# Weight sums of late mixed squares made early by GpSimd, and an eighth mixed square in six groups

## The chip, the cores and the metric

The kernel runs on one core of a Trainium2 chip. The metric is the device time of one execution in microseconds (us), and lower is better. A time stated here without a word beside it is the median of several executions. Times with a place in them ("at 982.89") are counted from the first instruction of one profiled execution.

The engines are named as the profile names them: PE is TensorE (matmuls; PEld its weight loads), DVE is VectorE, ACT is ScalarE, POOL is GpSimd, and SP is SyncE, which here only issues DMAs.

## The reference

One transformer block over 256 tokens of width 4096, in float32:

```python
h = _rmsnorm(x, norm_w)
u = h @ w_in                       # 4096 x 15,440: q, k, v, gates of two mixers
y_ml = rms(mlstm(...)) * sigmoid(ml_o) * silu(ml_z)
y_ns = nsa(...) * silu(ns_z)       # compressed, selected and window attention
x = x + concat([y_ml, y_ns]) @ w_out           # 4096 x 4096
x = x + sigmoid(x @ ple_gate) * (p @ ple_proj)  # 4096 x 4096
```

Nearly all of the arithmetic is in three large products with 256 rows of activations. Everything below is about those.

## The kernel before, in words

**Splits.** Each float32 operand is split into a high part that the fast matmul takes exactly, and a low part, the rest. A product is then three matmuls: high by high, low by high, high by low. The activations ("stationary", tiles `ss0` to `ss7`, `sh` and `sl`) are split once per stage. Each weight tile is loaded by SP into a buffer `raw` (six of them, 128 x 1024 numbers, 512 KB), ACT copies it to `whi` (line 1546, or 1556 for half a tile), and DVE subtracts to get `wlo` (line 1549, or 1559).

**Units.** The whole program is a list of 982 units, one weight tile each, and one loop (from line 1619 on) runs over it. While TensorE is given the matmuls of unit n, the low part of unit n + 3 and the high part of unit n + 4 are made; there are four `whi` and four `wlo`. Loads are issued as raw buffers come free (`load_some`, counted by `held_raw`). Between units, `step` takes one step each of three queues of generators (`urgent`, `fifo`, `third`), in which the attention, the recurrence, the evacuation of results and the preparation of the next activations are written out. All engines run their instructions in this order; only waits on data order them against each other.

**Pair groups and squares.** The weight columns are taken 1024 at a time in "pair groups" (`pair_group`): -9, -8, -7, -10 (early columns of w_in), -6 to -1 (its gate columns), 0 to 3 (w_out), 4 to 7 (ple_gate). The other columns of w_in are "wide groups" (`wide_group`, names such as nq2, 16 units of 12 matmuls each). A pair group has 16 squares kp = 0 to 15, each with 2 x 2 blocks of weights and 2 x 2 blocks of activations. A plain square ("C" in the plan) has two units of 12 matmuls: eight block products of three. A mixed square ("a" and, later, "c") uses seven products in place of eight, in the manner of Strassen and Winograd: units of 3, 6, 6 and 6 matmuls, 21 in all. It needs sums of the activation blocks (`cb`, made by `t_mix` or by `t_stat`) and sums of the weight blocks. Those are made in place, in the two raw buffers that the "a" units loaded, by `sums` (lines 1330, 1332, 1333 and 1335: four DVE additions of 128 x 512). The "c" units then split these sums, and until then the two raw buffers are held. "a" units split half a tile and then a whole one, "c" units two whole ones.

**Plans.** A plan lists the squares of a group. `FULL`, used by groups -5, -4, -3, -2, 1 and 2, has seven mixed squares, and in it 9 and 11 are open at once:

```python
FULL = _plan((0,), (3, 5, 7, (9, 11), 13, 1), (2, 4, 6, 8, 10, 12), (14, 15))
```

That is C0, a3 C2 c3, a5 C4 c5, a7 C6 c7, a9 a11 C8 c9 c11, a13 C10 c13, a1 C12 c1, C14, C15. `SIX` has six mixed squares (groups -9 and -7), and others have fewer.

**Buffers and queues that matter here.** `nat0` to `nat3` (128 x 2 x 1024) hold in turn the input for the norm, the shifted inputs of the compression, keys, mixed activations and the mixers' outputs y, and stand empty in between. `tb` (four small tiles) holds rows of the bias table, loaded on GpSimd's queue (line 520). GpSimd's queue also stores the result (line 1186). All weights go through SP's queue (line 1530), in order.

Of the kernel before, what the change touches and what calls it, by code (L numbers as in the profile page):

```python
# [55 lines left out]
MORE = 1  # L56
# [12 lines left out]
SIX = _plan((0, 1), MIXED, (2, 4, 6, 8, 10, 12), (14, 15))  # L69
TWICE = (3, (5, 7), 9, 11, (13, 1))  # L70
SHIFT = _plan((0,), TWICE, (2, 4, 6, 8, 10), (12, 14, 15))
PLANS = {g: FULL for g in (-5, -4, -3, -2, 1, 2)}
PLANS[-9] = PLANS[-7] = SIX
PLANS[-8] = _plan((0, 1, 2, 3), (5, 7, 9, 11, 13), (4, 6, 8, 10, 12), (14, 15))
CMP_AT = ((-8, 1), (-8, 3), (-8, 5), (-7, 1))
# [17 lines left out]
def hymba_block(ctx: ExitStack, tc: tile.TileContext, a, out: bass.AP):  # L93
# [713 lines left out]
    def mixed_tiles(kp, tag="b"):  # L807
        if tag == "e":
            if kp in (3, 7, 11):
                held["cb"] = wk.tile([128, 2, 2, 4, 128], F32R, tag={3: "a", 7: "nat2", 11: "nat3"}[kp], name="cb")  # L810
            t = held["cb"][:, int(kp in (5, 9, 13))]
            return t[:, 0], t[:, 1]
        if tag == "t":
            return [[wk.tile([128, 2, 128], F32R, tag="tb", name="cb", bufs=4) for _ in range(2)] for _ in range(2)]
        if kp == MORE:
            t = wk.tile([128, 2, 4, 128], F32R, tag="a" if tag == "b" else "b", name="cb")
        elif kp in (3, 5):
            t = wk.tile([128, 2, 4, 128], F32R, tag="qt", name="cb", bufs=2)
        elif kp == 7:
            t = wk.tile([128, 2, 4, 128], F32R, tag="sq", name="cb")  # L820
        elif kp == 13:
            return [wk.tile([128, 4, 128], F32R, tag="pt", name="cb", bufs=2) for _ in range(2)]
        else:
            if kp == 9:
                held["cb"] = wk.tile([128, 2, 2, 4, 128], F32R, tag=tag, name="cb")
            t = held["cb"][:, int(kp == 11)]
        return t[:, 0], t[:, 1]
# [4 lines left out]
    def t_mix(kps, flag, tag="b", gap=0):  # L832

        f = {}
        for i in range(len(kps) + 1):
            if i:
                nc.vector.tensor_sub(cb[kps[i - 1]][1], f[i - 1], cb[kps[i - 1]][0])
                done.add(f"{flag}{kps[i - 1] // 2}m")
            if i == len(kps):
                return  # L840
            c, b = kps[i] // 2, 2 * (kps[i] % 2)
            v = f[i] = stile([128, 4, 128])
            nc.vector.tensor_add(v.rearrange("p a t -> p (a t)"), sh[c][:, b:b + 2].rearrange("p k t -> p (k t)"),
                                 sl[c][:, b:b + 2].rearrange("p k t -> p (k t)"))
            nc.vector.tensor_sub(v[:, 3:0:-2], v[:, 1::-1], v[:, 3:0:-2])
            nc.vector.tensor_sub(v[:, 0], v[:, 0], v[:, 3])
            nc.vector.tensor_sub(v[:, 2], v[:, 2], v[:, 0])
            for _ in range(1 + gap):
                yield
            cb[kps[i]] = mixed_tiles(kps[i], tag)  # L850
            nc.scalar.activation(cb[kps[i]][0], v, AF.Copy)
            for _ in range(1 + gap):
                yield

# [5 lines left out]
    def t_stat(chunks, weighted, bset=1, pace=2, pause=0):  # L860


        def chunk(c, col0, gate, flag):
# [10 lines left out]
            for half in range(2):  # L874
                p, hs = pp[half], slice(2 * half, 2 * half + 2)
                w = [hnw[:, col0 // 128 + 2 * half + i:col0 // 128 + 2 * half + i + 1] for i in range(2)] if scales else None
                if 2 * c + half in MIXED or flag in (f"y{MORE // 2}", f"r{MORE // 2}") and half == MORE % 2:
                    f[half] = stile([128, 4, 128])
                    if scales:
                        for i in range(2):  # L880
                            nc.scalar.activation(f[half][:, 2 * i:2 * i + 2].rearrange("p a t -> p (a t)"), p[:, i],
                                                 AF.Copy, scale=w[i])
                        nc.scalar.activation(sh[c][:, hs].rearrange("p k t -> p (k t)"),
                                             f[half].rearrange("p a t -> p (a t)"), AF.Copy)
                        continue
                    nc.scalar.activation(f[half].rearrange("p a t -> p (a t)"), p.rearrange("p a t -> p (a t)"), AF.Copy)
                if scales:
                    for i in range(2):
                        nc.scalar.activation(sh[c][:, 2 * half + i], p[:, i], AF.Copy, scale=w[i])
                else:  # L890
                    nc.scalar.activation(sh[c][:, hs], p, AF.Copy)
# [360 lines left out]
    def pair_group(g, w, stat):  # L1252
# [125 lines left out]
            unit(w[kp, k], split, mm, kp, post=post)  # L1378

        def a_units(kp):  # L1380
            def split1(r):
                raw[kp] = [r]
                return split_one(r)

            def split2(r):
                raw[kp].append(r)
                low = split_all(r, keep=True)

                def rest():
                    hl = low()  # L1390
                    sums(kp, 0)
                    opened.extend(((kp, 1), (kp, 2)))
                    return hl
                return rest

            def mm1(hi, lo):
                emit(product(oth[0], blocks(kp)(0, 0), stream(hi, 0), stream(lo, 0)))

            def mm2(hi, lo):
                both(product(own[0][0], mixed(kp, 2), stream(hi, 0), stream(lo, 0)),  # L1400
                     product(own[0][1], blocks(kp)(1, 0), stream(hi, 1), stream(lo, 1)))
            unit(w[kp, 0], split1, mm1, kp, True)
            unit(w[kp, 1], split2, mm2, kp, True)

        def c_units(kp, last):
            def mm1(hi, lo):
                both(product(oth[3], mixed(kp, 1), stream(hi, 0), stream(lo, 0)),
                     product(oth[1], mixed(kp, 3), stream(hi, 1), stream(lo, 1)))

            def mm2(hi, lo):  # L1410
                both(product(oth[2], mixed(kp, 0), stream(hi, 0), stream(lo, 0)),
                     product(own[1][1], blocks(kp)(1, 1), stream(hi, 1), stream(lo, 1)))

            def post():
                finish(kp)
                if last:
                    urgent.append(t_x1_oth(g, oth) if 0 <= g < 4 else t_out_oth(g, oth, us))
                    if g in (-1, 3):
                        new_activations(g, range(2), 0)
            unit(None, lambda _: split_and_sum(raw[kp][0], kp), mm1)  # L1420
            unit(None, lambda _: split_and_sum(raw[kp][1], kp), mm2, post=post)

# [57 lines left out]
        def end():  # L1480
            if fin:
                fin()
            if g < -6:
                urgent.append(t_early_own(g, own, us))
            elif g < 0:
                urgent.append(t_gate_own(g, own, us))
            elif g < 4:
                urgent.append(t_x1_own(g, own))
            else:
                urgent.append(t_out_own(g, own, us, pj[0]))  # L1490
            if g in (-1, 3):
                new_activations(g, range(2, 8), 1)
            if g == 1:
                add(t_p())
            if g == -6:
                add(t_mix((MORE,), "x", "a", 3))
        units[-1]["post"] = end

    done.update(f"{n}{c}" for n in "ex" for c in range(8))
    for name in ORDER:  # L1500
        if name == "small":
            small_group()
        elif name in EARLY:
            pair_group(name, a["w_early"][list(EARLY).index(name)], "e")
            if name == -10:
                evq.extend(("oth-10", "oth-10"))
        else:
            wide_group(name, a["w_in"][WIDE.index(name)], None, p1_post(name))
    for g in range(-6, 0):
        pair_group(g, a["w_gate"][g + 6], "x")  # L1510
    for g in range(4):
        pair_group(g, a["w_out"][g], "y")
    for g in range(4, 8):
        pair_group(g, a["ple_gate"][g - 4], "r")


    raws, splits = {}, {}
# [1 line left out]
    def load(n):  # L1519
# [7 lines left out]
            for j in range(2):  # L1527
                nc.sync.dma_start(raws[n][:, j], units[n]["src"][:, j])
        else:
            nc.sync.dma_start(raws[n], units[n]["src"])  # L1530
        if n in XN:
            j = XN.index(n)
            nat[j] = wk.tile([128, 2, 1024], F32, tag=f"nat{j}", name=f"xn{j}")
# [17 lines left out]
            return hi, lo  # L1551
        return low

    def split_one(r):
        hi, lo = split_tiles()
        nc.scalar.activation(cols(hi, 0), cols(r, 1), AF.Copy)  # L1556

        def low():
            nc.vector.tensor_sub(cols(lo, 0), cols(r, 1), cols(hi, 0))  # L1559
            return hi, lo  # L1560
        return low

# [46 lines left out]
    def load_some():  # L1609
        while loads and held_raw[0] < RAWB:  # L1610
            held_raw[0] += 1
            load(loads.popleft())

    load_some()
    add(t_tables(), t_rms())
    for n in range(LOOK):
# [4 lines left out]
    for n in range(N):  # L1621
        if n + LOOK < N:
            split_low(n + LOOK)
        while behind:
            behind.popleft()()
        load_some()
        un = units[n]
        if un["pre"]:
# [12 lines left out]
        if n >= 3:  # L1641
            step([fifo])
            step([third])
    while step():
        pass

# [86 lines left out]
```

## Time and profile before

| | us |
|---|---|
| Runs: median of 3 (lowest to highest) | 2001.28 (2001.24 to 2001.41) |
| The profiled execution | 2001.38 |
| Its span, first to last instruction | 1999.6 |
| Busy: PE / DVE / ACT / POOL | 1992.0 / 1721.1 / 1212.9 / 23.3 |

The granted TensorE clock is 0.999 of full speed on average, so no throttling enters. In the profile, a line of the chain gives the start, the length and what ran; a line of the groups gives source line, engine, operation, output and inputs, shapes and count, then after the bar the busy time in us and the mean of one in ns, then the idle time of that engine just before such instructions and what ended it. A "q" behind an engine is its queue. Matmul lengths in the records overlap; their pace is read from start to start. A line of the waits gives who waited for whom, the total in us, how often, and the longest.

### The profile page before, as it was taken

The numbers are of one execution on the slowest core, as the hardware profiler recorded it, in microseconds if no ns is written. First come the engines' busy times: TensorE is split into PE (matmuls) and PEld (weight loads), VectorE is DVE, ScalarE is ACT, GpSimd is POOL, SyncE is SP. The second block draws the span as 40 slices with busy tenths as digits, with TensorE's granted clock in tenths as the row PEclk, the third lists the DMA queues.
The fourth block names the chain that finished last, engine by engine and source line by source line (L and its number), as shares of the span: only waits on it lengthen the run. The fifth ranks groups of instructions, "written<-read, shape, count | busy, mean of one in ns | idle before, by whom it ended". The sixth has DMA issues, their size and how long they took to land.

```text
span 1999.6 us, 26932 instructions
## 1 busy us (share of the span) xinstructions
PE 1992.0 (100%) x9594; PEld 1737.6 (87%) x9594; DVE 1721.1 (86%) x2235; ACT 1212.9 (61%) x1584; POOL 23.3 (1%) x59
## 2 busy tenths in 40 slices
PE   9999999999999999999999999999999999999998
PEld 8888888888888888888888888888888888888887
DVE  7797779787677776879999999999999998999988
ACT  7655556556666646566666666666555566656655
POOL 0000000000000000000000000000000000000000
PEclk9999999999999999999999999999999999999999
DMA  9666767575545455646666667565767674767664
GB/s 373 237 199 230 259 232 248 165 240 182 165 151 167 151 191 170 202 153 212 217 208 222 213 210 240 189 223 184 245 219 231 231 241 161 239 204 247 197 238 156
DMA packets 119351, 422.08 MB, mean 211 GB/s; under 512 B 14583, under 2 KB 14991, under 8 KB 119216
## 3 DMA queue, kind: packets, MB, share of 16 engines
q1 hardware_dynamic: 116880, 413.90, 61.9%
q0 software_dynamic: 2144, 6.44, 1.2%
q8 instruction: 75, 1.23, 0.2%
q14 instruction: 60, 0.49, 0.1%
q10 hardware_dynamic: 192, 0.02, 0.0%
HBM read 416.08 MB, written 4.23 MB: 210 GB/s over the span
## 4 chain that ended last, share of the span: by engine, by line
PE 99%; DVE 0%; ACT 0%; issue 0%; DVEq 0%; ACTq 0%
PE mm L1249 36%; PE sd L1249 34%; PE mm L971 14%; PE mm L973 7%; PE sd L640 1%; PE mm L1083 1%; PE sd L870 1%; PE sd L629 1%; PE sd L275 0%; PE mm L1059 0%; PE sd L580 0%; PE sd L596 0%; PE sd L595 0%; PE sd L594 0%; PE sd L153 0%; PE mm L870 0%
## 5 line engine op out<-in xcount | busy, mean ns | idle before, releaser
L1546 ACT ACTIVATE whi<-raw 128x1024 fp32r<-128x1024 f32 x852 | 889.7, 1055 | 670.4 <-DVE raw L1335 147.8
L1549 DVE TENSOR_TENSOR wlo<-raw,whi 128x1024 fp32r<-128x1024 f32 x852 | 1035.3, 1221 | 185.4 <-ACT whi L1546 174.2
L1249 PE MATMUL mm<-whi,ss 128*128 128x512 f32 x1794 | 492.3, 380 | 0.0
L1249 PE MATMUL sd<-whi,ss 128*128 128x512 f32 x1716 | 474.7, 380 | 0.0
L1249 PEld LDWEIGHTS mm<-whi,ss 128*128 128x128 f32 x1794 | 338.4, 189 | 47.3 <-issue 0.4
L1249 PEld LDWEIGHTS sd<-whi,ss 128*128 128x128 f32 x1716 | 323.9, 189 | 46.4 <-ACT whi L1546 0.4
L971 PE MATMUL mm<-whi,ss 128*128 128x512 f32 x1280 | 335.3, 385 | 0.0
L1249 PE MATMUL mm<-wlo,ss 128*128 128x512 f32 x897 | 280.6, 380 | 0.0
L1249 PE MATMUL sd<-wlo,ss 128*128 128x512 f32 x858 | 270.5, 380 | 0.0
L971 PEld LDWEIGHTS mm<-whi,ss 128*128 128x128 f32 x1280 | 237.5, 190 | 32.5 <-issue 1.6
L1249 PEld LDWEIGHTS mm<-wlo,ss 128*128 128x128 f32 x897 | 169.3, 189 | 24.9 <-DVE wlo L1549 1.4
L973 PE MATMUL mm<-wlo,ss 128*128 128x512 f32 x640 | 190.4, 379 | 0.0
L1249 PEld LDWEIGHTS sd<-wlo,ss 128*128 128x128 f32 x858 | 161.9, 189 | 24.1 <-DVE wlo L1549 1.7
L1249 PE MATMUL mm<-whi,cb 128*128 128x512 f32 x446 | 141.2, 379 | 0.0
L973 PEld LDWEIGHTS mm<-wlo,ss 128*128 128x128 f32 x640 | 121.2, 189 | 17.1
L1249 PE MATMUL sd<-whi,cb 128*128 128x512 f32 x426 | 136.1, 379 | 0.0
L1249 PEld LDWEIGHTS mm<-whi,cb 128*128 128x128 f32 x446 | 84.4, 189 | 11.9
L1249 PEld LDWEIGHTS sd<-whi,cb 128*128 128x128 f32 x426 | 80.6, 189 | 11.3
L1556 ACT ACTIVATE whi<-raw 128x512 fp32r<-128x512 f32 x109 | 67.6, 620 | 27.3 <-PE mm L1249 12.6
L1559 DVE TENSOR_TENSOR wlo<-raw,whi 128x512 fp32r<-128x512 f32 x109 | 74.7, 686 | 8.1 <-ACT whi L1556 8.0
L1333 DVE TENSOR_TENSOR raw<-raw 128x512 f32<-128x512 f32 x109 | 75.4, 692 | 3.8
L1249 PE MATMUL mm<-wlo,cb 128*128 128x512 f32 x223 | 75.5, 380 | 0.0
(315 smaller groups left out, 1496.6 us busy)
## 6 DMA issues: line engine op xcount, KB each, us to landing
raw<-in_w_gate SPq DMA_DIRECT2D x192, 512.0 KB, 4.2
raw<-in_w_in SPq DMA_DIRECT2D x159, 512.0 KB, 4.0
raw<-in_w_early SPq DMA_DIRECT2D x128, 512.0 KB, 4.2
raw<-in_w_out SPq DMA_DIRECT2D x128, 512.0 KB, 4.4
raw<-in_ple_gate SPq DMA_DIRECT2D x128, 512.0 KB, 4.3
raw<-in_w SPq DMA_DIRECT2D x16, 512.0 KB, 5.2
u<-in_xt SPq DMA_DIRECT2D x16, 256.0 KB, 7.5
xn<-in_x SPq DMA_DIRECT2D x4, 1024.0 KB, 9.7
```

The lines of the kernel that those rows point to most:

```text
L629: nc.tensor.transpose(psd[i][:, b, s, :], sb[i][:, b, s * 128:(s + 1) * 128], idn)
L640: MM(o[t][:, h, :], ptb[i][:, b, s, :], v[:, s, b, g * 128:(g + 1) * 128], start=False, stop=(i == 6 + t and b == 1 and s == t))
L870: nc.tensor.transpose(pp[i // 2][:, i % 2, t * 128:(t + 1) * 128], src[:, t, k:k + 128], idn)
L971: MM(box["ps"][t], s[c][:, k, t * 128:(t + 1) * 128], stream(m, j), start=st, stop=False)
L973: MM(box["ps"][t], sh[c][:, k, t * 128:(t + 1) * 128], stream(lo, j), start=False, stop=last)
L1083: MM(o[64 * kv:64 * kv + 60], xq[l // 8][:, l % 8, 60 * kv:60 * kv + 60], raw[:, j, 256 * kv:256 * kv + 256], start=l in (0, 24), stop=l i ...
L1249: MM(acc.t, s, m, start=acc.i == 0, stop=acc.i == acc.n - 1)
L1333: nc.vector.tensor_add(cols(r, 0), cols(r, 0), cols(r0, 1))
L1546: nc.scalar.activation(hi, r, AF.Copy)
L1549: nc.vector.tensor_sub(lo, r, hi)
L1556: nc.scalar.activation(cols(hi, 0), cols(r, 1), AF.Copy)
L1559: nc.vector.tensor_sub(cols(lo, 0), cols(r, 1), cols(hi, 0))
```

## The change

Three things change together.

1. Six groups (-5, -4, -3, -2, 1, 2) get the plan `EIGHT`: square 15 becomes mixed as well, and the order is C0, a3 C2 c3, a5 a7 C4 c5 c7, a9 a11 C6 c9 c11, a13 C8 c13, a1 a15 C10 c1 c15, C12, C14. The mixed activations of square 15 go to `tb` tiles, in two halves each; they are made at the end of group -6 by `t_mix`, and for groups 1 and 2 in the chunk of `t_stat` that also makes the activations 14 and 15.
2. For 19 mixed squares (7, 11 and 15 of the six groups, and 5 of group -5) the weight sums are no longer made in place. Their "a" units load half a tile (256 of 512 columns a row) and a whole one, give the raw buffers back at once, and their "c" units load the finished sums from a DRAM tile `stash`.
3. The sums are made early, in 38 jobs of half a square. `begin_sums(n)` has SP load 512 KB into a half of an empty `nat` tile; three units later `end_sums` has GpSimd make four additions of 128 x 256 and store the tile to `stash` from its own queue. The jobs' places are counted in units from the start of nq2: nine in `nat1` from -81 to -48 (in group -7), four in `nat2` from -13 to -3 (in group -10), sixteen in `nat3` from 1 to 52 and nine in `nat1` from 81 to 108 (in the wide groups).

```diff
+EXTRA = 15
+EIGHT = _plan((0,), (3, (5, 7), (9, 11), 13, (1, EXTRA)), (2, 4, 6, 8, 10), (12, 14))
+PLANS = {g: EIGHT for g in (-5, -4, -3, -2, 1, 2)}
+STASH = [(-5, 5)] + [(g, kp) for g in (-5, -4, -3, -2, 1, 2) for kp in (7, 11, EXTRA)]
...
-        if tag == "t":
+        if tag == "t" or kp == EXTRA:
             return [[wk.tile([128, 2, 128], F32R, tag="tb", name="cb", bufs=4) for _ in range(2)] for _ in range(2)]
...
         def a_units(kp):
+            ready = (g, kp) in stash
+
             def split1(r):
+                if ready:
+                    return split_one(r, False)
                 raw[kp] = [r]
                 return split_one(r)
 
             def split2(r):
+                if ready:
+                    return split_and_sum(r)
...
-            unit(w[kp, 0], split1, mm1, kp, True)
+            unit(w[kp, 0][:, :, 256:512] if ready else w[kp, 0], split1, mm1, kp, True)
             unit(w[kp, 1], split2, mm2, kp, True)
...
+            if (g, kp) in stash:
+                for i, mm in enumerate((mm1, mm2)):
+                    unit(stash[g, kp][i], split_and_sum, mm, post=post if i else None)
+                return
             unit(None, lambda _: split_and_sum(raw[kp][0], kp), mm1)
...
-                add(t_mix((MORE,), "x", "a", 3))
+                add(t_mix((MORE,), "x", "a", 3), t_mix((EXTRA,), "x", "a", 3))
...
+    stash = {key: drp.tile([2, 128, 2, 512], F32, name=f"sums{i}") for i, key in enumerate(STASH)}
...
+    jobs, begun = deque((key, h) for key in STASH for h in range(2)), deque()
+    times = [("nat1", t) for t in np.linspace(-81, -48, 9)] + [("nat2", t) for t in (-13, -10, -6, -3)]
+    times += [("nat3", t) for t in np.linspace(1, 52, 16)] + [("nat1", t) for t in np.linspace(81, 108, 9)]
+    times = deque((tag, begins["nq2"] + int(t)) for tag, t in times)
+    room = {}
+
+    def begin_sums(n):
+        if not times or n < times[0][1]:
+            return
+        tag, _ = times.popleft()
+        (g, kp), h = key = jobs.popleft()
+        if tag not in room or n > room[tag][2] + 20:
+            room[tag] = [0, wk.tile([128, 2, 2, 512], F32, tag=tag, name="job"), n]
+        r = room[tag][1][:, room[tag][0]]
+        room[tag][0] ^= 1
+        room[tag][2] = n
+        nc.sync.dma_start(r, weights[g][kp, :, :, h].rearrange("k p c -> p k c"))
+        begun.append((n + 3, key, r))
+
+    def end_sums(n):
+        if begun and n >= begun[0][0]:
+            _, (key, h), r = begun.popleft()
+            b = [r[:, k, 256 * j:256 * j + 256] for k in range(2) for j in range(2)]
+            for to, of in ((1, 0), (0, 2), (2, 1), (3, 2)):
+                nc.gpsimd.tensor_add(b[to], b[to], b[of])
+            nc.gpsimd.dma_start(stash[key][:, :, h].rearrange("k p c -> p k c"), r)
...
         while behind:
             behind.popleft()()
+        begin_sums(n)
         load_some()
...
             step([third])
+        end_sums(n)
```

The lines left out let `t_stat` and the last subtraction of `t_mix` work on two halves and include square 15 for the w_out stage, and load the half tile into the right half of a raw buffer.

More of the change, by code (lines that the diff above doesn't have):

```diff
@@ L71 @@
 SHIFT = _plan((0,), TWICE, (2, 4, 6, 8, 10), (12, 14, 15))
-PLANS = {g: FULL for g in (-5, -4, -3, -2, 1, 2)}
+EXTRA = 15
+EIGHT = _plan((0,), (3, (5, 7), (9, 11), 13, (1, EXTRA)), (2, 4, 6, 8, 10), (12, 14))
+PLANS = {g: EIGHT for g in (-5, -4, -3, -2, 1, 2)}
+STASH = [(-5, 5)] + [(g, kp) for g in (-5, -4, -3, -2, 1, 2) for kp in (7, 11, EXTRA)]
 PLANS[-9] = PLANS[-7] = SIX
@@ L836, in t_mix @@
             if i:
-                nc.vector.tensor_sub(cb[kps[i - 1]][1], f[i - 1], cb[kps[i - 1]][0])
+                hi, lo = cb[kps[i - 1]]
+                for (to, of), (h, _) in zip(runs(lo, f[i - 1]), runs(hi, f[i - 1])):
+                    nc.vector.tensor_sub(to, of, h)
                 done.add(f"{flag}{kps[i - 1] // 2}m")
@@ L850, in t_mix @@
             cb[kps[i]] = mixed_tiles(kps[i], tag)
-            nc.scalar.activation(cb[kps[i]][0], v, AF.Copy)
+            for to, of in runs(cb[kps[i]][0], v):
+                nc.scalar.activation(to, of, AF.Copy)
             for _ in range(1 + gap):
@@ L876, in chunk @@
                 w = [hnw[:, col0 // 128 + 2 * half + i:col0 // 128 + 2 * half + i + 1] for i in range(2)] if scales else None
-                if 2 * c + half in MIXED or flag in (f"y{MORE // 2}", f"r{MORE // 2}") and half == MORE % 2:
+                if 2 * c + half in MIXED + (MORE,) * (flag[0] in "yr") + (EXTRA,) * (flag[0] == "y"):
                     f[half] = stile([128, 4, 128])
@@ L1495, in end @@
             if g == -6:
-                add(t_mix((MORE,), "x", "a", 3))
+                add(t_mix((MORE,), "x", "a", 3), t_mix((EXTRA,), "x", "a", 3))
         units[-1]["post"] = end
+    weights = {g: a["w_gate"][g + 6] if g < 0 else a["w_out"][g] if g < 4 else a["ple_gate"][g - 4] for g in range(-6, 8)}
+    stash = {key: drp.tile([2, 128, 2, 512], F32, name=f"sums{i}") for i, key in enumerate(STASH)}
+    begins = {}
     done.update(f"{n}{c}" for n in "ex" for c in range(8))
     for name in ORDER:
+        begins[name] = len(units)
         if name == "small":
@@ L1508, in hymba_block @@
             wide_group(name, a["w_in"][WIDE.index(name)], None, p1_post(name))
[L1509 to L1514, printed above, removed]
+    begins[-6] = len(units)
+    for g, w in weights.items():
+        pair_group(g, w, "x" if g < 0 else "y" if g < 4 else "r")
     raws, splits = {}, {}
@@ L1529, in load @@
         else:
-            nc.sync.dma_start(raws[n], units[n]["src"])
+            src = units[n]["src"]
+            nc.sync.dma_start(cols(raws[n], 1) if src.shape[-1] == 256 else raws[n], src)
         if n in XN:
@@ L1552, in split_all, with split_one @@
         return low
-    def split_one(r):
+    def split_one(r, keep=True):
         hi, lo = split_tiles()
@@ L1559, in low @@
             nc.vector.tensor_sub(cols(lo, 0), cols(r, 1), cols(hi, 0))
+            held_raw[0] -= not keep
             return hi, lo
@@ L1643, in hymba_block @@
             step([third])
+        end_sums(n)
+    assert not jobs and not begun
     while step():
```

## The prediction

> **What bounds the kernel now.** I read the page first (busy shares, then the chain that ended last), then the busy time by stretches, then the chain and the waits inside the groups that the change touches.
>
> ```profile
> span 1999.6 us, 26932 instructions
> PE 1992.0 (100%) x9594; PEld 1737.6 (87%) x9594; DVE 1721.1 (86%) x2235; ACT 1212.9 (61%) x1584; POOL 23.3 (1%) x59
> PE 99%; DVE 0%; ACT 0%; issue 0%; DVEq 0%; ACTq 0%
> GB/s 373 237 199 230 259 232 248 165 240 182 165 151 167 151 191 170 202 153 212 217 208 222 213 210 240 189 223 184 245 219 231 231 241 161 239 204 247 197 238 156
> ```
>
> TensorE is the bound from end to end: the last chain is 99% matmuls. GpSimd does nothing to speak of. The execution took 2001.38 us, 1.8 us more than its span, and the runs' median is 2001.28. So time can only fall by fewer matmuls, or by the few places where TensorE waits. The chain in order of time shows both, here around groups -5 and -4:
>
> ```profile
> 970.59 6.47 PE sd L1249 x30
> ...
> 982.89 6.58 PE sd L1249 x30
> ...
> 1012.13 5.18 PE mm L1249 x24
> ...
> 1090.59 5.18 PE sd L1249 x24
> ```
>
> Thirty matmuls take 6.47 us, 0.2157 us each. The last two rows are the starts of groups -4 and -3: a group takes 78.46 us. The old plan has 7 mixed squares of 21 matmuls (3, 6, 6, 6 in its four units) and 9 plain ones of 24, in all 363, which by that pitch take 78.30. The difference is mostly in one piece, 6.58 instead of 6.47. Its cause is in the waits of 934 to 1327 us (groups -5 to -1):
>
> ```profile
> PEld mm L1249 <- DVE wlo L1549: 1.1, 4, 0.4
> PEld sd L1249 <- DVE wlo L1549: 0.8, 3, 0.4
> ```
>
> VectorE hands over a low part just too late there. It is the second limit, as the stretches say (columns after the window: its length, then PE, PEld, DVE, ACT, POOL busy with counts, clock, DMA share, GB/s). The first four are those in which the new jobs will run, the last two hold the six changed groups:
>
> ```profile
> 285.00:346.00 61.00, 61.00 (x284) 53.47 (x284) 55.63 (x63) 36.48 (x39) 3.32 (x6) 1.00 0.69 227
> 416.00:442.00 26.00, 26.00 (x122) 22.77 (x122) 23.19 (x27) 16.04 (x18) 0.00 (x0) 1.00 0.78 265
> 444.00:618.00 174.00, 174.00 (x922) 152.42 (x921) 121.34 (x205) 108.44 (x209) 4.93 (x10) 1.00 0.53 169
> 714.00:803.00 89.00, 89.00 (x425) 78.29 (x425) 63.66 (x111) 50.22 (x78) 4.62 (x12) 1.00 0.59 189
> 934.00:1327.00 393.00, 393.00 (x1826) 343.15 (x1825) 375.98 (x438) 244.66 (x270) 0.00 (x0) 1.00 0.64 214
> 1414.00:1571.00 157.00, 157.00 (x728) 137.29 (x727) 150.38 (x175) 90.27 (x96) 0.00 (x0) 1.00 0.70 232
> ```
>
> VectorE is 96% busy in both of the last two, and TensorE never idle.
>
> **The eighth square.** Square 15 was plain and becomes mixed in six groups: 24 matmuls become 21. That removes 6 x 3 = 18 matmuls, all on the path: 18 x 0.2157 = 3.88 us.
>
> **VectorE and ScalarE in the six groups.** From the groups by line, 934 to 1327 us:
>
> ```profile
> L1549 DVE TENSOR_TENSOR wlo<-raw,whi 128x1024 fp32r<-128x1024 f32 x195 | 236.7, 1220 | 11.4 <-ACT whi L1546 9.1
> L1333 DVE TENSOR_TENSOR raw<-raw 128x512 f32<-128x512 f32 x35 | 24.2, 692 | 1.2
> L1332 DVE TENSOR_TENSOR raw<-raw 128x512 f32<-128x512 f32 x35 | 24.0, 685 | 0.0
> L1559 DVE TENSOR_TENSOR wlo<-raw,whi 128x512 fp32r<-128x512 f32 x34 | 23.3, 686 | 3.5 <-ACT whi L1556 3.5
> L1546 ACT ACTIVATE whi<-raw 128x1024 fp32r<-128x1024 f32 x196 | 203.9, 1054 | 140.4 <-DVE raw L1335 50.3 <-DVE raw L1332 40.3 <-PE sd L1249 20.1
> L1556 ACT ACTIVATE whi<-raw 128x512 fp32r<-128x512 f32 x34 | 21.0, 618 | 7.3 <-PE mm L1249 3.8 <-PE sd L1249 3.4
> L843 DVE TENSOR_TENSOR s<-ss 128x512 f32<-128x512 f32 x1 | 0.7, 680 | 0.0
> L845 DVE TENSOR_TENSOR s<-s 128x256 f32<-128x256 f32 x1 | 0.4, 426 | 0.0
> L846 DVE TENSOR_TENSOR s<-s 128x128 f32<-128x128 f32 x1 | 0.3, 291 | 0.0
> ```
>
> A plain square costs VectorE two low parts, 2 x 1.22 = 2.44 us. A mixed one costs 0.69 + 3 x 1.22 = 4.35, and its four weight sums 4 x 0.69 = 2.74 more. With the sums of 7, 11 and 15 read back from DRAM, a group changes by +1.91 for square 15 and -2.74 for each of 7 and 11: -3.6 us of about 75. Without the stored sums it would be +4.65, and 75 + 4.65 is over the 77.6 us that 360 matmuls leave: the stash is what makes the eighth square affordable. ScalarE gets 0.62 + 1.05 = 1.67 us more per group at 62%: hidden behind TensorE.
>
> The mixed activations of square 15 are new work of the same kind as rows 843 to 846 and a last subtraction like the 0.69 ones: 0.68 + 0.43 + 2 x 0.29 + some 0.8 in halves, 2.5 us once in group -5 (which loses another 2.74 us of sums, its square 5), and 1.8 once at the end of group -1, where group 0 begins with seven plain squares. I cost both at nothing on the path; uncovered they would be 4.3 us.
>
> What goes with this is the late low part, 0.11 us a group. With 3.6 us less VectorE work I expect it to be gone: 6 x 0.11 = 0.66. The bounds are 0 and 0.8.
>
> **The loads of the stored sums.** A stashed square loads 0.25 + 3 x 0.5 MB where it loaded 1 MB, and no longer holds two raw buffers across a plain square. Its 21 matmuls take 4.53 us, and 1.84 million bytes in 4.53 us would be 405 GB/s, above the 373 GB/s of the page's first slice. Taken alone it is 0.4 us late, 19 x 0.4 = 7.4 us at worst. But the squares beside it load little: in "a9 a11 C6 c9 c11" the units carry 3.75 MB in 14.2 us (277 GB/s), and at most two of the six raw buffers are held where (9, 11) held four. I take 0.
>
> **The early sums.** 38 jobs, each a 512 KB load on SP's queue, four GpSimd additions of 128 x 256, a 512 KB store from GpSimd's queue. No row shows a GpSimd addition. The nearest:
>
> ```profile
> L443 POOL MEMSET hp<- 128x1024 f32 x1 | 1.0, 956 | 88.7 <-PE sd L1249 88.7
> L547 POOL MEMSET sc<- 128x256 f32 x4 | 1.3, 334 | 0.0
> L1186 POOL DMA_DIRECT2D out_x<-u x6 | 4.4, 729 | 1123.2 <-DVE u L1185 1123.2
> L520 POOL DMA_DIRECT2D tb<-rext_d x16 | 8.6, 541 | 329.9 <-DVE s L605 324.6 <-PE sd L580 5.3
> raw<-in_w_early SPq DMA_DIRECT2D x128, 512.0 KB, 4.2
> out_x<-u POOLq DMA_DIRECT2D x6, 512.0 KB, 4.9
> ```
>
> An addition of 128 x 256 lies between VectorE's 0.43 us for the same shape and three streams of the 0.334 us fill, 1.0 us; I take 0.6, nearer to the row of the same operation. Then 152 additions are 91 us of an engine with 1% use.
>
> Two queues are passed. On SP's, a job's load waits until its half of the buffer is stored, and the raw loads stand behind it. One pass is 4.2 (load) + 4 x 0.6 + 0.73 + 4.9 (store) = 12.2 us; a half comes round after two jobs, in group -7 after 2 x 53/8 = 13.3 us (nine jobs between units 81 and 48 ahead of nq2, 285 to 338 us by the rows below). It fits with 1 us to spare; at 1.0 us an addition SP is 0.5 us late each time, which the raw tiles in hand cover. On GpSimd's queue, an addition waits for its load, and the attention's table loads (L520) stand behind it. Those are issued two heads ahead, so 2.4 us of additions are hidden.
>
> ```profile
> 287.36 6.47 PE mm L1249 x30
> ...
> 355.35 10.36 PE sd L1249 x48
> ...
> L971 PE MATMUL mm<-whi,ss x1024: 378/379/568, 440.6 to 846.0; 128*128 128x512 f32 x171
> ```
>
> The first of these begins with the second unit of square 3 in group -7, which is unit 143; the second is the start of group -10, unit 182; the third gives the first matmul of nq2, unit 222. So unit 141 (222 - 81) is two units ahead of 287, and unit 174 lies eight units, 18 us, ahead of 355. The added traffic, 38 x 1 MB and 19 x 0.75 MB, is 55 MB on 422, in stretches that run at 169 to 265 GB/s. I take 0 for both queues, and 0.3 us in all for what small waits this crowding makes.
>
> **The sum.** 3.88 + 0.66 - 0.3 = 4.2 us; 2001.38 - 4.2 = 1997.2 for the profiled execution, 1997.1 for the median. About 0.2% (4.0 us) is what a measurement of this kernel can tell from no change, and this forecast lies right beside that line.
>
> **Rival 1, slower: GpSimd's additions take time from VectorE.** Nearly all of VectorE's work in 285 to 346 us reads two operands from SBUF, as a GpSimd addition does. If the two exclude each other, the nine jobs there (36 additions, 21.6 us) must find room in 61.0 - 55.6 = 5.4 us: 16.2 us too much. In 416 to 442 the four jobs need 9.6 us of 2.8: 6.8 too much. VectorE's look-ahead of three units takes off some 4 us in each. In the other two stretches there is room (52.7 us for 38.4, 25.3 for 21.6). TensorE would stand 12 + 3 = 15 us, less the gain: 2012. With 0.43 us an addition it is 6 + 0, 2003; the change loses from a stall of 4.2 us on. For it: those stretches are 91% and 89% busy. Against it: in the rows before, GpSimd never adds, so nothing shows that they exclude each other.
> By the Trainium skill, "SBUF — State Buffer", section "Who interferes with whom", a VectorE instruction with two SBUF inputs contends with a GpSimd instruction that reads SBUF, and the one that starts second is blocked entirely; no run so far shows it. By that rule the time is this rival's. The Trainium skill's "GPSIMD Engine Reference", section "Performance versus the Vector engine", gives 4497 ns for an addition of 2048 elements, which by length would be 0.56 us here (an estimate from that page).
>
> **Rival 2: crowded transfers or handshakes eat the gain.** Part of the 7.4 us of late stashed loads, or SP held behind a job's buffer, comes out as stall: with 3 of them, 2000. For it: nine jobs leave SP only 1 us per pass. Against it: the largest rate in the touched stretches is 265 GB/s.
>
> **The numbers.** Forecast 0.50, rival 1 0.33, rival 2 0.17. The forecast's own range is 1996.6 to 1998.0, from 4.7 us with all waits gone to 3.3. Seven tenths of it lie beyond 0.2%: faster 0.35. Same is the rest of it and most of rival 2: 0.27. Slower is rival 1 and the tail of rival 2: 0.38. The range reaches to 2012, the middle of rival 1, and leaves out its dearer half.
>
> **What would show it.** Right: 360 matmuls between starts of groups -4 and -3, 77.7 us; no 6.58 piece; the wlo rows at 1.22 us while GpSimd adds; the four early stretches as long as before. Wrong: VectorE rows that grow longer or TensorE waits for wlo in 285 to 346 us (rival 1), or ScalarE waiting for DMA in the six groups and SP for GpSimd (rival 2).

## The result, and the profile after

| | before | after |
|---|---|---|
| Runs side by side: median (lowest to highest), us | 2001.35 (2001.24 to 2001.85) | 2013.17 (2010.77 to 2015.22) |
| Ratio, 95% interval | | 1.0058 (1.0041 to 1.0076) |
| The profiled execution, us | 2001.38 | 2013.3 |
| Its span, us | 1999.6 | 2011.5 |

One execution of an experiment below (short fills) took 4286 us where its nine others took 2003 to 2006, and its ratio leaves that one out.

The change makes the kernel 11.8 us slower. The forecast was 4.2 us faster; rival 1 gave 2012. The page of after, its span, busy times, chain and the new line of GpSimd:

```profile
span 2011.5 us, 27251 instructions
PE 1993.8 (99%) x9576; PEld 1732.3 (86%) x9576; DVE 1739.5 (86%) x2205; ACT 1227.6 (61%) x1601; POOL 215.6 (11%) x249
...
PE 93%; DVE 3%; issue 1%; DMA 1%; POOL 1%; ACT 0%; DVEq 0%; POOLq 0%; ACTq 0%; SPq 0%
...
L1658 POOL TENSOR_TENSOR job<-job 128x256 f32<-128x256 f32 x152 | 164.0, 1079 | 358.7 <-DMA job<-in_w_gate 233.1
```

The 18 matmuls are gone (9576 in place of 9594), but the chain is no longer TensorE's alone. VectorE ran 30 instructions fewer and was busy 18.4 us longer, so its instructions grew. The same stretches as before show where (the last moved by the 14 us that the groups start later):

```profile
285.00:346.00 61.00, 56.44 (x246) 44.89 (x245) 60.02 (x52) 29.86 (x32) 41.48 (x34) 1.00 0.84 290
416.00:442.00 26.00, 26.00 (x122) 22.80 (x121) 24.55 (x24) 17.11 (x18) 8.94 (x8) 1.00 0.78 251
444.00:618.00 174.00, 171.56 (x895) 149.18 (x895) 128.05 (x192) 104.82 (x195) 84.47 (x97) 0.99 0.80 275
...
948.00:1341.00 393.00, 391.30 (x1818) 341.20 (x1817) 365.44 (x416) 254.58 (x281) 0.00 (x0) 1.00 0.72 241
```

In the first row VectorE has 60.02 of 61 us full and gets 52 instructions done, where it did 63 in 55.63. TensorE gets 246 matmuls in place of 284. The groups of VectorE in that stretch, by form:

```profile
L1568 DVE TENSOR_TENSOR wlo<-raw,whi 128x1024 fp32r<-128x1024 f32 x26 | 38.5, 1488 | 0.8 <-ACT whi L1565 0.7
L1578 DVE TENSOR_TENSOR wlo<-raw,whi 128x512 fp32r<-128x512 f32 x5 | 5.5, 1108 | 0.0
L1336 DVE TENSOR_TENSOR raw<-raw 128x512 f32<-128x512 f32 x5 | 5.5, 1106 | 0.0
```

The low part takes 1.49 us on average (1.22 before), the half 1.11 (0.69). The waits of TensorE's weight loads and of SP's queue in the same stretch:

```profile
PEld mm L1255 <- DVE wlo L1568: 7.3, 9, 1.6
...
SPq L1650 <- DMA sums<-job: 21.8, 5, 6.8
```

TensorE waits for low parts; and SP, with the weights of the group behind it in its queue, stands 21.8 us at the jobs' loads until a half of the buffer is stored. Which of the two TensorE feels, VectorE's own waits tell: were the raw tiles late, ScalarE's high parts would be, and VectorE would stand idle for them. Here it hardly does (before: 5.9 us, the same row with the old line numbers):

```profile
DVE wlo L1568 <- ACT whi L1565: 0.7, 1, 0.7
```

Lengths of the groups in the profiled executions, each from its first matmul with a low part to that of the next, worked out from the traces (us more than before; an empty place is under 0.1; "six" is the sum over -5, -4, -3, -2, 1 and 2):

| | -7 | -10 | nq2 | nq3 | mq0 and mk0 | mk1 | six |
|---|---|---|---|---|---|---|---|
| before, length | 82.79 | 85.46 | 44.91 | 55.32 | 112.82 | 43.63 | 470.83 |
| after | +9.05 | | +3.04 | +1.42 | +0.77 | | -1.57 |
| no additions | +0.99 | | | | | | -0.28 |
| 20 fills | +6.10 | | | | | +5.46 | -1.96 |
| 11 fills | +3.61 | | | | | | -1.75 |
| two additions | +2.57 | | +0.92 | | | | -1.56 |
| nothing loaded again | +15.19 | | +2.65 | +0.76 | +0.25 | | -0.74 |

The other stretches of after come to -0.8 us, most of it at the very start. These are single executions. Jobs alone (below) runs the same instructions as the kernel after up to group -6, and its -7, nq2 and nq3 were 0.8, 1.2 and 1.2 us shorter; so about 1 us in one group can be chance.

Group -4 is the clean case; the chain has its start and that of -3, 77.70 us apart (78.46 before):

```profile
1026.17 5.18 PE mm L1255 x24
...
1103.87 5.18 PE sd L1255 x24
```

So the late low part did go where nothing disturbed a group. But groups -5, -2 and 1, with one late low part each, take 78.77, 78.94 and 78.45 us, 0.75 to 1.24 over the 77.70. In 948 to 1341 us ScalarE now waits for loads, and TensorE for low parts:

```profile
ACT whi L1565 <- DMA raw<-in_w_gate: 10.2, 16, 1.6
...
ACT whi L1565 <- DMA raw<-sums: 1.5, 2, 1.3
PE mm L1255 <- DVE wlo L1568: 0.9, 1, 0.9
...
PE sd L1255 <- DVE wlo L1568: 0.8, 1, 0.8
```

Before, the waits for loads were 3.1 us in all. The last two rows are the late low parts of groups -2 and -5.

### The profile page after: what moved, and what is told of

Same layout as the page of the kernel before. It is cut to its first block, busy times and chain, and to the rows that moved or that the text cites. A ratio compares the mean times of both kernels' runs of the same rounds, so it can differ in the third digit from the quotient of the medians.

```text
span 2011.5 us, 27251 instructions
## 1 busy us (share of the span) xinstructions
PE 1993.8 (99%) x9576; PEld 1732.3 (86%) x9576; DVE 1739.5 (86%) x2205; ACT 1227.6 (61%) x1601; POOL 215.6 (11%) x249
## 4 chain that ended last, share of the span: by engine, by line
PE 93%; DVE 3%; issue 1%; DMA 1%; POOL 1%; ACT 0%; DVEq 0%; POOLq 0%; ACTq 0%; SPq 0%
PE mm L1255 34%; PE sd L1255 33%; PE mm L977 12%; PE mm L979 6%; DVE wlo L1568 1%; PE sd L643 1%; DMA job<-in_w_gate 1%; PE mm L1089 1%; POOL job L1658 1%; PE sd L876 1%; PE sd L632 1%; PE sd L278 0%; PE mm L1065 0%; DVE raw L1336 0%; PE sd L583 0%
## 5 line engine op out<-in xcount | busy, mean ns | idle before, releaser
L1568 DVE TENSOR_TENSOR wlo<-raw,whi 128x1024 fp32r<-128x1024 f32 x858 | 1054.5, 1240 | 182.7 <-ACT whi L1565 172.7
L1255 PE MATMUL sd<-whi,ss 128*128 128x512 f32 x1686 | 468.7, 380 | 0.0
L1255 PEld LDWEIGHTS sd<-whi,ss 128*128 128x128 f32 x1686 | 318.1, 189 | 45.6 <-issue 0.8
L1658 POOL TENSOR_TENSOR job<-job 128x256 f32<-128x256 f32 x152 | 164.0, 1079 | 358.7 <-DMA job<-in_w_gate 233.1
L1255 PE MATMUL mm<-whi,cb 128*128 128x512 f32 x470 | 148.8, 379 | 0.0
L1255 PE MATMUL sd<-whi,cb 128*128 128x512 f32 x450 | 143.7, 379 | 0.0
L1578 DVE TENSOR_TENSOR wlo<-raw,whi 128x512 fp32r<-128x512 f32 x115 | 80.9, 704 | 7.8 <-ACT whi L1575 7.6
```

Source lines behind the costliest of these rows:

```text
L1255: MM(acc.t, s, m, start=acc.i == 0, stop=acc.i == acc.n - 1)
L1568: nc.vector.tensor_sub(lo, r, hi)
L1658: nc.gpsimd.tensor_add(b[to], b[to], b[of])
```

## The experiments

Two theories stood. **Port theory** (rival 1): GpSimd's additions and VectorE's instructions with two operands in SBUF exclude each other. **Queue theory** (part of rival 2): SP is held behind the jobs' half buffers, and GpSimd's queue holds the attention's work. Each kernel ran beside the kernel before on the same chip, whose median there was between 2001.75 and 2001.93; the ratios are taken to that.

### The additions left out

```diff
-            for to, of in ((1, 0), (0, 2), (2, 1), (3, 2)):
-                nc.gpsimd.tensor_add(b[to], b[to], b[of])
```

> The changed kernel without GpSimd's 152 additions; each job still loads its tile and stores it, so what the c units of the 19 squares read are unsummed weights. Port theory (a GpSimd addition and a VectorE operation with two SBUF inputs exclude each other): group -7 is back at 82.8 us from 91.8, VectorE's wlo rows are back at 1.22 us, and the time is 1999 to 2002 us. Queue theory (SP stands with the raw loads behind it until a job's half buffer is stored): the wait shrinks by the 3 to 5 us of the additions alone, so group -7 keeps 3 to 6 us of its 9, and the time is 2005 to 2009 us.

Measured: 2000.65 us, ratio 0.9996 (0.9986 to 1.0006), no difference from before. All loads and stores of the jobs are still there. The stretch of 285 to 346 us, and its low parts:

```profile
285.00:346.00 61.00, 60.55 (x280) 52.39 (x279) 53.59 (x60) 34.55 (x37) 5.52 (x8) 1.00 0.94 339
```
```profile
L1568 DVE TENSOR_TENSOR wlo<-raw,whi 128x1024 fp32r<-128x1024 f32 x31 | 37.8, 1222 | 8.5 <-ACT whi L1565 8.1
```

The additions are the cause of nearly all of the loss, and the transfers, at 339 GB/s here, of 1 us at most. But with the loss gone, the gain of 4.2 us is not there either: the interval ends at 2.8 us.

### Fills in place of additions

```diff
-            for to, of in ((1, 0), (0, 2), (2, 1), (3, 2)):
-                nc.gpsimd.tensor_add(b[to], b[to], b[of])
+            for i in range(20):
+                nc.gpsimd.memset(b[i % 4], 1.0)
```

> The changed kernel with 20 GpSimd fills of 128 x 256 in the place of the four additions, so that GpSimd is busy about as long per job (some 5 us) and SP waits as long, but GpSimd only writes; the stored tiles hold ones. Port theory, if it is the read side that is shared: VectorE's rows stay at 1.22 us in 285 to 346 us and the time is 1999 to 2004 us. Queue theory, or any GpSimd access excluding VectorE: as the changed kernel, 2011 to 2015 us.

Measured: 2013.02 us, ratio 1.0054 (1.0039 to 1.0069); the profiled execution had 2010.32. A job's fills took 5.1 us, about as long as the disturbed additions. They write to SBUF and read nothing. The stretch, its low parts and SP's wait:

```profile
285.00:346.00 61.00, 58.85 (x266) 50.81 (x264) 50.80 (x57) 31.96 (x34) 40.45 (x147) 0.97 0.83 296
```
```profile
L1568 DVE TENSOR_TENSOR wlo<-raw,whi 128x1024 fp32r<-128x1024 f32 x28 | 34.2, 1222 | 10.0 <-ACT whi L1565 9.7
```
```profile
SPq L1650 <- DMA sums<-job: 29.4, 5, 8.9
```

GpSimd was as busy as in the kernel after (40.45 us), and VectorE's low parts stayed at 1222 ns: a GpSimd instruction that only writes does not hold them up. VectorE had 10.2 us free. Still group -7 lost 6.1 us, because SP stood at the buffers and the raw tiles came late. Not all of that is the wait itself: the clock of 0.97 stands for 3.41 us at half clock after one wait (last section), a loss of some 1.7 us that the kernel after does not have in this group. So the queue is a cost of its own at this length of a pass, about 4.4 us by this estimate.

The 5.5 us of mk1 are something else. Fills and VectorE's instructions there:

```profile
738.37 5.14 POOL L1658 MEMSET job<- 128x256 f32 x20 [3.52 <-DMA job<-in_w_out]
...
739.67 3.98 DVE L698 TENSOR_SCALAR sq<-u,convw_c 128x256 f32<-128x256 f32 x1
...
745.03 5.13 POOL L1658 MEMSET job<- 128x256 f32 x20
...
746.27 4.04 DVE L698 TENSOR_SCALAR sq<-u,convw_c 128x256 f32<-128x256 f32 x1
```

Line 698 takes 0.35 us (median of 16). Three of them began during a run of fills, took 4.0 to 4.6 us, and ended when the fills did. So fills do hold up one kind of VectorE instruction: this one, which reads one tile and a column of factors. A low part came 3.5 us late by it, and a second stretch of half clock followed. In group -7 no instruction of VectorE grew.

### Fills as long as undisturbed additions

```diff
+            for i in range(11):
+                nc.gpsimd.memset(b[i % 4], 1.0)
```

> The changed kernel with eleven GpSimd fills of 128x256 (about 2.8 us, as long as four additions that nothing disturbs) in place of a job's four additions; the stored sums are then constants and not the reference's. The loads and stores of the jobs stay. The fills read nothing, so the port theory expects VectorE's rows at 1.22 us and group -7 at 83 to 84.5 us, the whole 2001 to 2003 us. The theory that SP's standing behind the buffers is a cost of its own at this length too expects 86 to 88 us in group -7 and 2005 to 2010 us.

Measured: 2004.72 us, ratio 1.0015 (1.0005 to 1.0025). A job's fills take 2.8 us, four additions at their shortest, 0.717 us, 2.9:

```profile
285.00:346.00 61.00, 59.32 (x268) 49.59 (x267) 51.28 (x58) 31.88 (x34) 24.80 (x84) 1.00 0.87 303
```
```profile
L1568 DVE TENSOR_TENSOR wlo<-raw,whi 128x1024 fp32r<-128x1024 f32 x29 | 35.4, 1222 | 11.1 <-ACT whi L1565 10.7
```

Group -7 loses 3.6 us with VectorE undisturbed and the clock at 1.00: in that stretch VectorE waits 10.7 us for high parts, where it waited 0.7 in the kernel after. The group is where the queue theory put it, the whole 0.3 us below its range. Behind group -7, in the wide groups, nothing is lost. So even if the two engines had not met, the queue of group -7 would have cost about 3.6 us that the forecast put at 0.

### SP not held

```diff
-        nc.sync.dma_start(r, weights[g][kp, :, :, h].rearrange("k p c -> p k c"))
+        if not 29 <= len(jobs) <= 35:
+            nc.sync.dma_start(r, weights[g][kp, :, :, h].rearrange("k p c -> p k c"))
```

> The changed kernel, but of the nine jobs in group -7 only the first two load their weights, one into each half of the buffer; the other seven add and store what already stands there (their sums are not the reference's). SP then has no load that waits for a half of the buffer to be stored; the 36 additions and nine stores in group -7 stay. Port theory (the additions and VectorE's two-operand instructions exclude each other): group -7 still takes 90.5 to 92 us, and the whole 2011 to 2014 us. Queue theory (SP stands behind the jobs' buffers, and the raw tiles come late): group -7 falls to 83 to 84.5 us, the whole to 2003 to 2006. Between these, both have a share, and group -7's length gives it.

Measured: 2019.17 us, ratio 1.0088 (1.0071 to 1.0105).

```profile
285.00:346.00 61.00, 52.55 (x225) 40.74 (x223) 59.98 (x47) 25.77 (x28) 48.17 (x41) 1.00 0.74 245
```
```profile
L1568 DVE TENSOR_TENSOR wlo<-raw,whi 128x1024 fp32r<-128x1024 f32 x23 | 37.7, 1648 | 0.8 <-ACT whi L1565 0.8
```

SP no longer waits for a store in this stretch, and the group loses 15.2 us instead of 9.05. This falls on the port theory's side and beyond its numbers: the low parts take 1.65 us. With no load to wait for, GpSimd adds without a pause. In the kernel after, the slow pass through the buffer had spread the nine jobs over 290 to 364 us; here they run from 290 to 351. So the two costs do not add: the queue limits how densely the engines meet.

### Half of the additions, and copies

```diff
-            for to, of in ((1, 0), (0, 2), (2, 1), (3, 2)):
+            for to, of in ((1, 0), (3, 2)):
```

> The changed kernel with two of the four additions of each job (the stored sums are not the reference's). Port theory: all 36 additions of group -7 took 9.05 us and the 5.4 us that VectorE had free there, 14.4 us; half of them take 7.2, of which 5.4 are free: group -7 takes 84 to 85.5 us, the early groups behind it lose 1 to 2 us in place of 5.3, and the whole is 2002 to 2005 us. If the loss goes by the number of jobs (their transfers and handshakes), group -7 stays at 89 to 92 us and the whole at 2010 to 2014.

Measured: 2004.08 us, ratio 1.0012 (1.0003 to 1.0021); group -7 +2.57, and low parts of 1316 ns. That is the dose that the port theory gave. It doesn't tell the theories apart, though: two additions at 1.3 us are as long as the eleven fills, which cost 3.6.

The other kernel has eight copies in place of the four additions:

```diff
+            for to, of in ((1, 0), (0, 2), (2, 1), (3, 2)) * 2:
+                nc.gpsimd.tensor_copy(b[to], b[of])
```

> The changed kernel with eight GpSimd copies of 128x256 in place of a job's four additions (the stored values are not the reference's sums). A copy reads one operand from SBUF where an addition reads two. If any GpSimd instruction that reads SBUF excludes VectorE's two-operand instructions, the rows of the low parts grow beyond 1.35 us in 285 to 346 us as with the additions, and group -7 takes 87 to 93 us. If only a GpSimd instruction with two operands does, the rows stay at 1.22 us, group -7 takes 83 to 86 us and the whole 2001 to 2005 us.

Measured: 2016.41 us, ratio 1.0073 (1.0058 to 1.0088). Group -7 takes 92.49 us. The low parts of 285 to 346 us, and the copies over the whole run (shortest, median and longest in ns):

```profile
L1568 DVE TENSOR_TENSOR wlo<-raw,whi 128x1024 fp32r<-128x1024 f32 x27 | 36.4, 1361 | 4.9 <-ACT whi L1565 4.9
```
```profile
L1658 POOL COPY job<-job x304: 394/402/1470, 289.6 to 822.0; 128x256 f32<-128x256 f32 x152
```

A copy reads one operand and disturbs VectorE as well (by 0.14 us a low part), and is itself held from 0.39 to as much as 1.47 us. One operand read from SBUF is enough. The loss of the group is another matter: VectorE waits 4.9 us for high parts here and SP stands 35.1 us at the jobs' loads, so the queue has a larger share in it than in the kernel after.

### The jobs alone, and the plan alone

One kernel keeps the old plan and runs the jobs for nothing; the other has the new plan, loads plain weights in place of the stored sums, and has no jobs:

```diff
-PLANS = {g: EIGHT for g in (-5, -4, -3, -2, 1, 2)}
+PLANS = {g: FULL for g in (-5, -4, -3, -2, 1, 2)}
...
-            ready = (g, kp) in stash
+            ready = False
```
```diff
-                    unit(stash[g, kp][i], split_and_sum, mm, post=post if i else None)
+                    unit(w[kp, i], split_and_sum, mm, post=post if i else None)
...
-        begin_sums(n)
...
-        end_sums(n)
```

> The old plans, with the 38 jobs running and nobody reading their sums. If the loss lies with the jobs, whichever way: group -7 takes 91.8 us, nq2 47.9, nq3 56.7, the six groups 78.45 each, and the time is 2001.3 + 9.0 + 3.0 + 1.4 + 0.9 = 2015.6 us (2013 to 2018). If the loss lay with the new plan or its DRAM reads: 2001 to 2003 us.

> The new plan without the jobs; the c units of the 19 squares load plain weights of the same size in the place of the sums. The change's own groups differ from before by +0.3, -0.75, -0.75, +0.36, 0 and -0.75 us, so 2001.3 - 1.6 - 0.3 = 1999.4 us (1998.8 to 2000). The prediction's term of 3.88 + 0.66 us would give 1996.8 us; it holds if the three late low parts of groups -5, -2 and 1 come from the jobs' reads of DRAM.

Measured: jobs alone 2014.48 us, ratio 1.0062 (1.0047 to 1.0077); group -7 takes 91.05 and the six groups 78.45 to 78.57 each, as before. The plan alone: 2001.93 us, ratio 1.0001 (0.9991 to 1.001). So the loss lies with the jobs. And the gain is missing with the plan by itself, where 1998.8 to 2000 was expected: in its profile, groups -4, -3, -2, 1 and 2 take 77.73, 78.69, 79.05, 78.59 and 78.62, four of them with a low part about 1 us late. Its waits of 944 to 1340 us:

```profile
ACT whi L1565 <- DMA raw<-in_w_gate: 13.6, 22, 3.1
...
PEld sd L1255 <- DVE wlo L1568: 2.7, 3, 1.2
PEld mm L1255 <- DVE wlo L1568: 2.3, 5, 1.3
```

### The queues, by other engines

The jobs' loads go out on GpSimd's queue; and in another kernel the attention's fill of `sc` (line 550) goes to VectorE:

```diff
-        nc.sync.dma_start(r, weights[g][kp, :, :, h].rearrange("k p c -> p k c"))
+        nc.gpsimd.dma_start(r, weights[g][kp, :, :, h].rearrange("k p c -> p k c"))
```
```diff
-        nc.gpsimd.memset(sc, 0.0)
+        nc.vector.memset(sc, 0.0)
```

> The changed kernel with the jobs' loads issued from GpSimd's queue, so that SP never waits for a job's buffer; the additions and the VectorE work are as they were. Port theory (the additions and VectorE's two-input operations exclude each other, and VectorE is full in group -7): group -7 keeps most of its 9 us (88 to 93 us long), VectorE's wlo rows stay near 1.45 us there, and the time is 2009 to 2014 us. Queue theory (the raw loads held behind the job's buffer make the stall): group -7 is at 83 to 84 us and the time 2001 to 2005 us.

> The changed kernel with the small fill of the score tile moved from GpSimd to VectorE, so that the attention does not stand behind a job in GpSimd's queue. If that queue makes the loss in nq2: nq2 is back from 47.9 to 45 to 45.5 us, no stretch of half clock follows at 497 us, and the time is 2.5 to 3 us below the changed kernel, 2010 to 2011 us. If the loss in nq2 is VectorE's (port): nq2 stays above 47 us and the time at 2013 us.

Measured: loads on GpSimd's queue 2040.97 us, ratio 1.0194 (1.018 to 1.0208). Neither theory had that. Group -7 loses only 2.3 us, but -10 loses 30.9. GpSimd's queue, in which the jobs now wait for their own loads too, has a fill for the attention (line 446) behind them; VectorE waits for that fill, and TensorE for what stands behind it in VectorE's queue:

```profile
DVE hp L458 <- POOL hp L446: 29.5, 1, 29.5
PEld mm L278 <- DVE u L396: 26.9, 1, 26.9
```

GpSimd did fewer additions in group -7 there, so its short length decides nothing between the theories. The moved fill: 2012.62 us, ratio 1.0052 (1.0038 to 1.0066); nq2 takes 46.57 in place of 47.95. In nq2 of the kernel after, the fill stood behind a job:

```profile
482.65 5.15 POOL L1658 TENSOR_TENSOR job<-job 128x256 f32<-128x256 f32 x4 [2.47 <-DMA job<-in_w_gate]
488.10 0.74 POOL L1659 DMA_DIRECT2D sums<-job  x1 [0.30 <-POOL job L1658]
488.84 0.33 POOL L550 MEMSET sc<- 128x256 f32 x1
```

The 1.4 us less in nq2 does not show that this queue costs time there. Jobs alone has the same fill behind a job, and its nq2 took 46.71; what the kernel after has beyond both is a stretch of half clock (last section). And with either number of fills in a job, the fill of `sc` behind them, nq2 is as long as before. What costs time in nq2 went with the additions.

### A smaller version

Thirty jobs, none in group -7; five groups with eight mixed squares (-5 keeps the old plan), the pairs behind two single squares; the mixed activations of square 15 made in group -4; the fill of `sc` on VectorE. The second kernel has the jobs' loads on GpSimd's queue besides.

```diff
-EIGHT = _plan((0,), (3, (5, 7), (9, 11), 13, (1, EXTRA)), (2, 4, 6, 8, 10), (12, 14))
-PLANS = {g: EIGHT for g in (-5, -4, -3, -2, 1, 2)}
+EIGHT = _plan((0,), (3, 5, (7, 9), (11, 13), (1, EXTRA)), (2, 4, 6, 8, 10), (12, 14))
+PLANS = {g: EIGHT for g in (-4, -3, -2, 1, 2)}
...
-    times = [("nat1", t) for t in np.linspace(-81, -48, 9)] + [("nat2", t) for t in (-13, -10, -6, -3)]
+    times = [("nat2", t) for t in (-13, -10, -6, -3)]
```

> A version meant to keep the gain: no jobs in group -7, 30 jobs for 15 squares, the new plan in five groups (-5 keeps the old one) with its pairs moved behind two single squares, the fill on VectorE, and the mixed activations of square 15 made in group -4. Port theory: group -7 is 82.8 us; VectorE's slack in the wide groups (30 and 27%) takes the additions, 0.5 to 2 us of stall; the five groups give 5 x 0.75 less one or two late loads of 1 us: 2001.3 - 3.75 - 0.3 + 1.5 + 1.2 = 1999.9 us (1998.2 to 2001.5). If additions cost time wherever they are: 8 us for the 30 jobs, 2005 us or more.

> The thirty-job version with the jobs' loads on GpSimd's queue. If SP's waits for a job's buffer cost something in the wide groups, this is 0.5 to 1.5 us faster than the thirty-job version (1998.5 to 1999.5 us); if they are covered there by the loads' lead, the same within 0.3 us.

Measured: 2003.17 us, ratio 1.0005 (0.9996 to 1.0014), no difference from before and above the expected range; with loads on GpSimd's queue 2006.32, ratio 1.0025 (1.0014 to 1.0036), slower where faster or the same was expected. With loads on SP's queue, group -7 has its 82.79 us back and nq2 takes 44.86. The six groups are together 1.7 us shorter in the profiled execution, which was the shortest (1999.39, the longest 2004.96): single late low parts come and go. With loads on GpSimd's queue, -10 and nq2 are 1.8 and 3.8 us longer than before. None of the versions beats the kernel before.

## Why the prediction was wrong

**The early sums, where it failed.** The forecast gave the 152 additions 0.3 us of crowding and took GpSimd as an idle engine. Rival 1 is what happened. GpSimd's additions and VectorE's two-operand instructions keep each other waiting: 0.717 us at the shortest and up to 1.805 for the one (estimated at 0.6), 1.22 to a mean of 1.49 for the other, and leaving the additions out brings the time back. The groups in which the jobs ran lost 14.3 us in place of the 0.3. By the Trainium skill, "SBUF — State Buffer", section "Who interferes with whom", this is so for a VectorE instruction with two SBUF inputs and a GpSimd instruction that reads SBUF, but not for one that only writes. The low parts of 1488 ns with additions, 1361 with copies and 1222 with fills agree. I gave that rule's result 0.33 because no row showed the meeting; the rows that did stand there, VectorE at 91% of 61 us with nearly all of it two-operand work, were enough to make it the forecast.

**SP's queue, which failed too.** I put it at 0: a pass of 12.2 us in 13.3. Three rows of one half's turns in the kernel after (the jobs between them used the other half):

```profile
290.32 5.84 POOL L1658 TENSOR_TENSOR job<-job 128x256 f32<-128x256 f32 x4 [83.16 <-DMA job<-in_w_gate]
...
310.13 6.22 POOL L1658 TENSOR_TENSOR job<-job 128x256 f32<-128x256 f32 x4 [4.85 <-DMA job<-in_w_gate]
...
325.64 5.95 POOL L1658 TENSOR_TENSOR job<-job 128x256 f32<-128x256 f32 x4 [1.52 <-DMA job<-in_w_gate]
```

A pass took 19.8 and 15.5 us. The additions of a job were about 5.8 in place of 2.4; the load and the store, medians 5.9 and 6.1 over the run, were 1.7 and 1.2 us longer than the rows of before from which I took them. With nothing but the fills' 2.8 us, it still cost 3.6 us: the raw tiles in hand did not cover it. In the kernel after, though, this is not what TensorE waited for, as VectorE's 0.7 us of waits for high parts show.

**Rival 1's own sum.** Its mechanism held. That its total, 15 us of stall for 2012, came out is in part luck, for its terms did not. Group -7 lost 9.05 and not 12, as the passes spread the additions (without SP's holds it loses 15.2; the rival had 16.2 before the look-ahead's part). Group -10 lost nothing, not 3. The wide groups, put at "there is room", lost 5.2: room on average did not help there. And the gain that the rival subtracted was 1.6 us in the six groups, not 4.2.

**The eighth square.** 18 matmuls less: right, 9576. The length of an undisturbed group, 77.7: right in -4, -3 and 2. The late low part of 0.11 us gone in all six: wrong. Three of them got a new one, and the six gave 1.57 us in place of 3.88 + 0.66. The plan brings this and not the jobs, as the plan alone shows it too. The traces say where each comes from. Those of -5 and -2 stand at the same place, 18.4 and 19.9 us into the group, and cost TensorE 0.8 and 0.9 us in the kernel after, without the additions and with the plan alone. In both, VectorE had run for 15 us or more without a gap. In -5 the mixed activations of square 15, put at nothing on the path, ran just ahead of the low part:

```profile
963.56 0.69 DVE L848 TENSOR_TENSOR s<-ss 128x512 f32<-128x512 f32 x1
...
965.07 0.29 DVE L852 TENSOR_TENSOR s<-s 128x128 f32<-128x128 f32 x1
965.28 3.49 DVE L1568 TENSOR_TENSOR wlo<-raw,whi 128x1024 fp32r<-128x1024 f32 x3
```

In -2 no single step explains it; with the pairs moved, in the smaller version, it was gone (77.82 us). In group 1 it is the loads, put at 0: ScalarE waited for stored sums, and VectorE then for ScalarE:

```profile
1451.27 1.06 ACT L1565 ACTIVATE whi<-raw 128x1024 fp32r<-128x1024 f32 x1 [1.44 <-DMA raw<-sums]
...
1454.92 1.23 DVE L1568 TENSOR_TENSOR wlo<-raw,whi 128x1024 fp32r<-128x1024 f32 x1 [0.73 <-ACT whi L1565]
```

Such late loads vary from kernel to kernel: with the plan alone, ScalarE's waits for gate weights came to 13.6 us, and -3 and 2 were late as well.

**What stays open** is a price for each of the two in group -7. Between 290 and 364 us VectorE stood waiting for high parts 2.3 us in the kernel after, 13.0 with the short fills; so nearly all of the 9.05 us came to TensorE through VectorE's lengthened work. But that work is as long as it is only because the engines meet as often as the queue lets them: without the holds they cost more. No run gives one share independent of the other.

## What to carry to other kernels

An engine at 1% is not free to use: look at which operands its instructions read and write, and which instructions the engine that is the second limit runs at that moment. A buffer that is reused puts its whole pass (load, work, store) into the queue of whoever loads it; cost that pass with the durations as they will be when everything runs at once, and add what stands behind it. Where a group's slack is 1 us, fewer matmuls are only worth their full time if every load, and every instruction of the second limit, still comes as early as before.

## What the runs showed of the hardware

A wait of 1.9 us of TensorE was followed by 3.4 us at half clock. In nq2 of the kernel after, TensorE stood still until 496.46 us (the wait in brackets), and the stretches of 4 us around it show the clock, the third number from the end:

```profile
496.46 0.41 PE L578 MATMUL sd<-idn,sc 128*128 128x128 f32 x2 [1.90 <-DVE sc L572]
```

```profile
489.00:493.00 4.00, 3.59 (x17) 2.84 (x16) 3.10 (x9) 2.35 (x6) 1.07 (x3) 1.00 1.03 379
493.00:497.00 4.00, 2.10 (x13) 1.61 (x12) 3.83 (x10) 2.62 (x7) 3.46 (x6) 1.00 0.89 342
497.00:501.00 4.00, 4.00 (x13) 3.20 (x12) 3.58 (x9) 3.05 (x8) 0.31 (x1) 0.57 0.88 245
501.00:505.00 4.00, 4.00 (x22) 3.53 (x21) 3.78 (x8) 2.81 (x9) 2.42 (x3) 1.00 1.02 380
```

The third row has 13 matmuls where the fourth has 22; 0.43 of 4 us, 1.7 us, come on top of the wait. By the trace's record of the clock it is 3.41 us at 0.50, from 497.31 on. The waits for low parts in 285 to 346 us, up to 1.6 us, left the clock at 1.00; with 20 fills, where one wait in that stretch was 2.5 us, it was 0.97:

```profile
PEld mm L1255 <- ACT whi L1565: 2.5, 1, 2.5
```

So a short wait of TensorE can cost twice, and the 3.0 us that nq2 lost hold such a second part. The length of the wait does not settle it: with nothing loaded again, a wait of 1.90 us that ended at 503.06 us left the clock at 1.00.
